# A hybrid decoder step: three feed-forwards of seven products, each behind the next group's mixing

## The chip, the cores and the metric

The kernel runs on one core of a Trainium2 chip, as one launch. The metric is the device time of that launch in microseconds (us). A core has five engines that run side by side and wait for each other through semaphores: TensorE (PE) multiplies matrices into PSUM banks, VectorE (DVE) and ScalarE (ACT) do elementwise work and may read PSUM, GpSimd (POOL) does elementwise work in SBUF only, and SyncE (SP) issues the DMA transfers. Each engine takes its instructions in the order of its own queue.

## The reference

A prompt of 2048 tokens and a sample group of 8 sequences of 8 tokens go through one decoder layer with the same weights (width 1024, feed-forward width 4096):

```
h    = rmsnorm(x)
proj = h @ w_in                      # 1024 x 4096: q, k, v, gate of 4 retention heads and of 4 HGRN2 heads
o    = per-head gated recurrence, head rmsnorm, swish gate
x    = x + o @ w_out                 # 1024 x 1024
x    = x + square(relu(rmsnorm(x) @ w_up)) @ w_down     # 1024 x 4096 and back
y    = rmsnorm(x)
```

The recurrence is computed in chunks; the prompt's state goes from one token group to the next, so the groups are mixed in order. The outputs are `y`, and the states of both kinds of heads after the prompt and after each sample sequence.

All of it is float32. The large products are made with operands split in two parts, `hi` (rounded to the matrix engine's input format) and `lo` (the rest): hi·hi + hi·lo + lo·hi, three matmuls in place of one.

## The kernel before, in words

Tokens lie on the free axis, channels on the 128 partitions. The 2112 tokens are worked on in three groups (`GROUPS`): 512 prompt tokens, then the 64 sample tokens with 768 prompt tokens (832), then 768 prompt tokens. For each group come, in this order, the mixing (`mix`: input projection, recurrence, gates), the output projection, and the feed-forward. The whole is one long emission in program order; PE works through it without a gap where the other engines keep up.

**The order of the work** is written by hand. Every matmul of a projection, or every second one of a feed-forward, calls `tick()`. `later(n, fn)` and `at(t, fn)` put other work (splits, sums, evacuations, loads) into an agenda that is carried out n ticks on, between the matmuls. `flush()` empties the agenda. `plan_sums` fills a second list, `side`, whose times are ticks too.

**Weights** come as tiles of 128 x 1024 from one array. `weight()` loads a tile (L241) into a buffer `raw`, ACT makes its `hi` part (L277), DVE or POOL its `lo` part (L292). In the first group the parts of all mixing and output weights but four are stored to DRAM (L325, `kept`), and the later groups load them back ready-made (L261).

**Two ways to do the feed-forward.** Group 0 (512 tokens, one piece of 512 columns) multiplies every weight block by its tokens: 64 weight tiles of 24 matmuls (`ffn_first`, `up_first`, `down_first`; the matmul is L352). Groups 1 and 2 cut the operands into 2 x 2 quarters and make seven products in place of eight (`ffn`, `up`, `down`; the matmul is the helper at L1146). A quarter is half of the group's tokens wide, so the matmuls have 416 and 384 columns. The seven products need sums of weight quarters S1 to S4: `plan_sums` loads quarters (L1286), adds them on DVE (L1289) and stores the sums to DRAM (L1294), for the up weights during group 0's feed-forward and for the down weights during group 1's mixing. They also need sums of token quarters T1 to T4 (`block_sum`, L1347), and each operand must be split (`halve`: L1336 on ACT, L1340 on DVE).

In `down` the result of a product goes from PSUM to SBUF by `put` (L1550 on DVE). Of the seven products of an octet some continue in the PSUM banks of the one before (`first` is false in `OCTET`), so that PE may go on in a bank only after DVE has read it:

```
OCTET = (("A11", "B11", True, ("U",)), ("A12", "B21", False, ((0, 0),)), ("S1", "T1", True, ((1, 1),)),
         ("S4", "B22", False, ((0, 1),)), ("S3", "T3", True, ((1, 1),)), ("A22", "T4", False, ((1, 0),)),
         ("S2", "T2", True, ("U",)))
```

Each product of `down` takes two weight tiles (v = 0 and 1) with a PSUM tile of two banks each, 24 matmuls a tile. The hidden activations go to DRAM after `up` and come back in `down`.

**Memory.** Most temporaries are slabs of 832 columns, 42 of them. PSUM holds two two-bank tiles `pj` for the large products and four single banks `mm`.

**Samples.** The 64 sample tokens are the first columns of group 1. `sample_update` (L771, L774) multiplies the keys by the values masked by sequence, in plain float32, and adds the result to the eight states of a head.

Of the kernel before, what the change touches and what calls it, by code (L numbers as in the profile page):

```python
# [9 lines left out]
F32 = mybir.dt.float32  # L10
# [5 lines left out]
P = 128  # L16
D = 1024
# [11 lines left out]
SLAB = 832  # L29
NSLAB = 42  # L30
# [6 lines left out]
GROUPS = ((0, 0, 512), (NS, 512, 768), (0, 1280, 768))  # L37
# [4 lines left out]
W_UP0 = W_OUT0 + N_OUT  # L42
W_DN0 = W_UP0 + N_UP
NQ = FF // (4 * P)
NO = NQ // 2

W_UQ0 = W_DN0 + N_DN
W_DQ0 = W_UQ0 + N_UP
NW = W_DQ0 + N_DN

# [41 lines left out]
NCONST = C_SM + NSEQ  # L92
# [14 lines left out]
def constants():  # L107
# [6 lines left out]
    for h, g in enumerate(GAM):  # L114
        dec = np.where(s <= t, g ** np.maximum(t - s, 0), 0.0) * sc
        c[:, C_RM + h * P:C_RM + (h + 1) * P] = dec
        c[:, C_RS + h * P:C_RS + (h + 1) * P] = np.where(same, dec, 0.0)
        c[:, C_GQ + h * P:C_GQ + (h + 1) * P] = g ** (t + 1.0)
        c[:, C_GS + h * NS:C_GS + (h + 1) * NS] = g ** (np.arange(NS) % SLEN + 1.0)
        c[:, C_KS + h] = sc * g ** (P - 1.0 - s[:, 0])  # L120
        c[:, C_KSS + h] = np.where(s[:, 0] < NS, sc * g ** (SLEN - 1.0 - s[:, 0] % SLEN), 0.0)
    c[:, C_SM:C_SM + NSEQ] = (s // SLEN == np.arange(NSEQ)[None, :])
# [31 lines left out]
def lay_out_weights(w_in, w_out, w_up, w_down):  # L154
# [14 lines left out]
    for ps in (range(0, H - 1), range(H - 1, H)):  # L169
        bl = [wo[kind, p, :, n] for n in N_ORDER for p in ps for kind in (1, 0)]  # L170
        for j in range(0, len(bl), 8):
            w[i] = np.stack(bl[j:j + 8], 1).reshape(P, WT)
            i += 1
    wu = w_up.reshape(KB, P, FF // P, P)
    for f in range(FF // P):
        w[i] = wu[:, :, f].transpose(1, 0, 2).reshape(P, WT)
        i += 1
    wd = w_down.reshape(8, 4, P, 4, 256)
    for f in range(8):
        for n in range(4):  # L180
            w[i] = wd[f, :, :, n].transpose(1, 0, 2).reshape(P, WT)
            i += 1
# [25 lines left out]
class Kernel:  # L208
# [43 lines left out]
    def weight(self, i):  # L252
        n = len(self.stream)
        while self.w_next < min(i + 1 + self.ahead, n):
# [39 lines left out]
    def plan_stream(self):  # L294

        self.stream = [("w", j) for j in range(W_UP0)]
        up = [[("w", W_UP0 + 4 * t + i) for i in range(4)] for t in range(NQ)]
        dn = [[("w", W_DN0 + 4 * t + i) for i in range(4)] for t in range(NQ)]
        self.stream += up[0]
        for t in range(NQ):  # L300
            self.stream += (up[t + 1] if t < NQ - 1 else []) + dn[t]
        self.n_first = len(self.stream)
# [3 lines left out]

        for g in range(1, len(GROUPS)):
            self.stream += [("p" if j >= N_MADE else "w", j) for j in range(W_UP0)]
# [3 lines left out]
            for o in range(NO):  # L312
                for k, (name, *_) in enumerate(LAST_OCTET if o == NO - 1 else OCTET):
                    end = g == len(GROUPS) - 1 and o == NO - 1 and k > 4
                    self.stream += [entry(name, ("d", o, v), W_DQ0 + 4 * (2 * o + v), not end and (2 * k + v) % 5 in (1, 3))
                                    for v in range(2)]

    def next_weight(self):
# [3 lines left out]
        if N_MADE <= i < W_UP0:  # L322
# [16 lines left out]
    def proj(self, g, blocks, acts, pieces=None):  # L339
# [3 lines left out]
        self.n_proj += 1  # L343
        if self.spread and self.n_proj % 3:
            pj = self.mm().unsqueeze(1)
        else:
            pj = self.pj.tile([P, 2, 512], F32, tag="pj", name="pj")
# [31 lines left out]
    def build(self):  # L379
        nc, tc, I = self.nc, self.tc, self.I  # L380
        with ExitStack() as ctx:
# [11 lines left out]
            self.ordered, self.spread, self.n_proj = True, False, 0  # L393
# [49 lines left out]
            for i, g in enumerate(gs):  # L443
                nxt = gs[i + 1] if i + 1 < len(gs) else None
                if i == 0:
                    self.mix(g)
                    self.plan_sums(sums[:NQ - 1], [90 + 200 * j for j in range(NQ - 1)])

                    self.spread = True
                    self.out_proj_first(g)  # L450
                    self.ffn_first(g, nxt)
                    self.spread = False
                    continue
                if i == 1:
                    self.finish_first(gs[0])

                    self.plan_sums(sums[NQ - 1:], [141 + 200 * (j // 2) + 85 * (j % 2) for j in range(2 * NO)])
                else:
                    self.finish(gs[i - 1])
                self.mix(g)  # L460
                self.out_proj(g)
                while self.side:
                    self.side.popleft()[1]()
                self.ffn(g, nxt)
# [64 lines left out]
    def norm_in(self, g, start=False):  # L529
# [71 lines left out]
        else:  # L601
            for kb in range(KB):
                self.later(5 * kb, piece, kb)
        t0 = 60 if start else 5 * KB
# [103 lines left out]
    def values(self, g, p, b):  # L708
# [7 lines left out]
        while left:  # L716
# [5 lines left out]
            for i, s in enumerate(part):  # L722
# [9 lines left out]
                if g.ns and s == 0:  # L732
                    b["vs"] = pair
# [29 lines left out]
    def sample_update(self, v, kt, s0, which, h, decay):  # L763
# [3 lines left out]
        for i in range(2):  # L767
            vm = self.get()
            v3 = vm[:, :512].rearrange("p (s v) -> p s v", v=P)
            m = self.con[:, C_SM + 4 * i:C_SM + 4 * i + 4]  # L770
            nc.vector.tensor_tensor(out=v3, in0=v.unsqueeze(1).to_broadcast([P, 4, P]),  # L771
                                    in1=m.unsqueeze(2).to_broadcast([P, 4, P]), op=ALU.mult)
            ps = self.mm()
            nc.tensor.matmul(ps, kt, vm[:, :512], start=True, stop=True)  # L774
# [24 lines left out]
    def mixer(self, g, p, b, t0):  # L799
# [181 lines left out]
        def turn(key, src, sg, cscale):  # L981

            scale = None if cscale is None else con[:, cscale + p:cscale + p + 1]
            if sg == 2:
                x[key, 2] = self.get()[:, :P]
                self.transposes(src, [slice(0, P)], x[key, 2], None if cscale is None else con[:, C_KSS + p:C_KSS + p + 1])
# [42 lines left out]
        def sample_state(hd):  # L1029
            last = x["eb"][:, :NS].rearrange("p (s j) -> p s j", j=SLEN)[:, :, SLEN - 1]  # L1030
            self.sample_update(b["vs"][hd], x["kth" if hd else "ktr", 2], x["s0", hd], hd, p, last if hd else GAM[p] ** SLEN)
# [62 lines left out]
        if n0:  # L1094
            at(t - 14, sample_load, 0)
            at(t + 1, sample, 0)
# [54 lines left out]
    def residual(self, g):  # L1151
# [4 lines left out]
        for n in N_ORDER:  # L1156
# [4 lines left out]
        self.flush()  # L1161
        return part

    def out_proj_first(self, g):
        nc, T = self.nc, g.T
        part = self.residual(g)
        acts = g.oc[H - 1]
        g.acc, h2 = [part[n] for n in range(KB)], {}  # L1170
        for n in N_ORDER:
            pj = self.proj(g, self.take(2), acts)
            acc, hi, lo = g.acc[n], self.getr(), self.getr()
            nc.vector.tensor_tensor(out=self.v2(acc, g), in0=pj, in1=self.v2(acc, g), op=ALU.add)
            wf = self.vec[:, V_FFN + n:V_FFN + n + 1]
            nc.scalar.activation(hi[:, :T], acc[:, :T], AF.Copy, scale=wf)  # L1176
            self.later(7, lambda acc=acc, hi=hi, lo=lo, wf=wf: nc.vector.scalar_tensor_tensor(
                out=lo[:, :T], in0=acc[:, :T], scalar=wf, in1=hi.bitcast(F32)[:, :T], op0=ALU.mult, op1=ALU.subtract))
            h2[n] = (hi, lo)
        g.h2 = [h2[n] for n in range(KB)]  # L1180

    def scale_residual_first(self, g):


        nc, T = self.nc, g.T
        x = {"sum": None}

        def square(acc):
            x["sum"] = self.add_square(g, x["sum"], acc)

        def split():
            x["parts"] = self.halves(g, x["sum"])

        def mean():
            x["q"] = self.get()
            for (c0, c1), ps in zip(g.pieces, self.both_sums(g, x["parts"])):
                nc.vector.tensor_scalar(out=x["q"][:, c0:c1], in0=ps, scalar1=1.0 / D, scalar2=EPS,
                                        op0=ALU.mult, op1=ALU.add)

        def scale(acc):  # L1200
            nc.gpsimd.tensor_tensor(out=acc[:, :T], in0=acc[:, :T], in1=x["q"][:, :T], op=ALU.mult)

        def guard():
            self.last_guard(g, x["q"])

        for n, acc in enumerate(g.acc):
            self.later(7 * n, square, acc)
            self.later(120 + 7 * n, scale, acc)
        self.later(92, split)
        self.later(112, mean)  # L1210
        self.later(194, guard)

    def up_first(self, g):
        nc, T = self.nc, g.T
        u = []
        for _ in range(4):
            pj = self.proj(g, self.take(KB), g.h2)
            r, hi, lo = self.get(), self.getr(), self.getr()
            nc.scalar.activation(self.v2(r, g), pj, AF.Relu)
            nc.scalar.activation(hi[:, :T], r[:, :T], AF.Square)  # L1220
            nc.vector.tensor_tensor(out=r[:, :T], in0=r[:, :T], in1=r[:, :T], op=ALU.mult)
# [598 lines left out]
```

## Time and profile before

| what | value |
|---|---|
| median of 3 runs | 2559.0 us (2558.8 to 2559.46) |
| the profiled execution | 2557.37 us |
| its span, first to last instruction | 2555.3 us |
| PE busy | 2533.7 us, 99% |
| DVE busy | 1677.7 us, 66% |
| ACT busy | 1167.0 us, 46% |
| POOL busy | 694.3 us, 27% |
| DMA | 442.33 MB, mean 173 GB/s |
| granted TensorE clock | 0.999 |

The rows that the prediction shows come from these views. The groups of instructions give, for a line and a shape, the count, the busy time (time that two instructions share is not counted twice), the mean duration of one, and the idle time of the engine before them with what ended it. A matmul's own duration is longer than its distance to the next, because matmuls overlap; what one costs in a stream is read from the starts in the timeline, where a row is `start, duration, engine, line, operation, tile, shape, count`. The windows give busy time of PE, PE's weight load, DVE, ACT and POOL in a stretch with the number of instructions in brackets, then the granted clock, the mean busy share of the 16 DMA engines, and GB/s. The waits of PE give total, times and longest.

### The profile page before, as it was taken

The page shows a single profiled execution, that of the slowest core. Times are in us where ns is not written, and L with a number is a line of the kernel's source. Part 1 is how long each engine was busy: PE and PEld are TensorE (multiplying, and loading weights), DVE is VectorE, ACT ScalarE, POOL GpSimd, SP SyncE. Part 2 cuts the span into 40 slices and gives each one's busy share as a digit, 9 for nine tenths or more (in the row PEclk, how much of TensorE's full clock was granted, in tenths as well). Part 3 has the DMA queues.
Part 4 walks back from the last instruction along what each step waited for, and adds up shares of the span by engine and source line. Part 5 has one row for each costly group of instructions (what it writes and reads, how often), then busy time and mean ns, then how long its engine had stood idle before and what let it go on. Part 6 is the DMA issues. An engine that isn't in the chain of part 4 may idle for free. (4 is left out here: it accounts for less than half of the span.)

```text
span 2555.3 us, 37138 instructions
## 1 busy us (share of the span) xinstructions
PE 2533.7 (99%) x14691; PEld 2401.3 (94%) x14691; DVE 1677.7 (66%) x2135; ACT 1167.0 (46%) x1570; POOL 694.3 (27%) x443
## 2 busy tenths in 40 slices
PE   8999999999999999999999999999999999999998
PEld 7888888888999999999999999999999999999998
DVE  6777775556657666665646978875456465549787
ACT  6776532325334434344434444544444354345444
POOL 4333241111324243202222322243243012222220
PEclk9999999999999999999999999999999999999999
DMA  7666854564264545644557555442222325565452
GB/s 269 217 220 225 291 198 173 189 215 133 91 231 149 198 170 167 244 132 161 169 169 245 188 173 180 145 153 83 109 106 96 120 85 188 174 215 205 173 181 91
DMA packets 146173, 442.33 MB, mean 173 GB/s; under 512 B 14672, under 2 KB 36176, under 8 KB 146000
## 3 DMA queue, kind: packets, MB, share of 16 engines
q1 hardware_dynamic: 145856, 439.94, 49.8%
q8 instruction: 116, 1.90, 0.3%
q14 instruction: 57, 0.47, 0.1%
q10 hardware_dynamic: 144, 0.02, 0.0%
HBM read 331.11 MB, written 108.79 MB: 172 GB/s over the span
## 5 line engine op out<-in xcount | busy, mean ns | idle before, releaser
L352 PE MATMUL pj<-slab,hi 128*128 128x416 f32 (+2 forms) x2844 | 740.1, 363 | 6.4 <-ACT hi L277 6.0
L277 ACT CAST hi<-raw 128x1024 fp32r<-128x1024 f32 x330 | 347.7, 1054 | 666.6 <-PE pu L1146 185.4
L352 PEld LDWEIGHTS pj<-slab,hi 128*128 128x128 f32 x2844 | 512.8, 188 | 39.3 <-ACT hi L277 6.3
L292 POOL TENSOR_TENSOR lo<-raw,hi 128x1024 fp32r<-128x1024 f32 x92 | 247.6, 2691 | 852.5 <-ACT hi L277 791.7
L1146 PE MATMUL pd<-slab,hi 128*128 128x416 f32 (+1 forms) x1776 | 464.8, 342 | 2.0 <-DVE slab L1550 2.0
L352 PE MATMUL pj<-slab,lo 128*128 128x416 f32 (+2 forms) x1422 | 434.4, 364 | 0.6 <-DVE lo L292 0.5
L292 DVE TENSOR_TENSOR lo<-raw,hi 128x1024 fp32r<-128x1024 f32 x238 | 301.7, 1268 | 199.5 <-ACT hi L277 199.0
L1146 PE MATMUL pu<-slab,hi 128*128 128x416 f32 (+1 forms) x1600 | 408.4, 342 | 0.0
L1146 PEld LDWEIGHTS pd<-slab,hi 128*128 128x128 f32 x1776 | 326.8, 188 | 4.9 <-issue 1.8
L1146 PE MATMUL pd<-slab,lo 128*128 128x416 f32 (+1 forms) x888 | 305.2, 344 | 0.0
L1146 PEld LDWEIGHTS pu<-slab,hi 128*128 128x128 f32 x1600 | 294.1, 188 | 1.5
L352 PEld LDWEIGHTS pj<-slab,lo 128*128 128x128 f32 x1422 | 259.5, 188 | 17.7 <-issue 1.9
L1146 PE MATMUL pu<-slab,lo 128*128 128x416 f32 (+1 forms) x800 | 264.2, 343 | 0.0
L352 PE MATMUL mm<-slab,hi 128*128 128x512 f32 x740 | 229.5, 390 | 0.0
L728 PE MATMUL pjv<-hi,slab 128*128 128x256 f32 x1088 | 212.4, 287 | 1.4 <-ACT slab L738 1.4
L1340 DVE TENSOR_TENSOR slab<-slab 128x832 fp32r<-128x832 f32 (+1 forms) x144 | 162.9, 1149 | 36.8 <-ACT slab L1336 17.6
L728 PEld LDWEIGHTS pjv<-hi,slab 128*128 128x128 f32 x1088 | 174.3, 190 | 3.8 <-ACT slab L738 2.2
L1336 ACT CAST slab<-slab 128x832 fp32r<-128x832 f32 (+1 forms) x144 | 122.5, 862 | 115.0 <-DVE slab L1347 83.0
L1146 PEld LDWEIGHTS pd<-slab,lo 128*128 128x128 f32 x888 | 166.6, 188 | 0.5
L352 PEld LDWEIGHTS mm<-slab,hi 128*128 128x128 f32 x740 | 138.5, 188 | 29.2 <-ACT slab L1176 0.4
L728 PE MATMUL pjv<-lo,slab 128*128 128x256 f32 x544 | 153.8, 283 | 0.0
L1146 PEld LDWEIGHTS pu<-slab,lo 128*128 128x128 f32 x800 | 149.6, 188 | 0.5
(207 smaller groups left out, 3666.6 us busy)
## 6 DMA issues: line engine op xcount, KB each, us to landing
raw<-w SPq DMA_DIRECT2D x270, 512.0 KB, 4.2
u<-ld SPq DMA_DIRECT2D x32, 416.0 KB, 4.2
slab<-u SPq DMA_DIRECT2D x32, 416.0 KB, 5.5
u<-ld SPq DMA_DIRECT2D x32, 384.0 KB, 4.6
slab<-u SPq DMA_DIRECT2D x32, 384.0 KB, 5.7
ld<-x SPq DMA_DIRECT2D x16, 416.0 KB, 6.4
ld<-x SPq DMA_DIRECT2D x16, 384.0 KB, 4.3
raw<-su1S SPq DMA_DIRECT2D x8, 512.0 KB, 4.6
```

Of the source, the lines that this page charges most:

```text
L277: self.nc.scalar.copy(hi, raw)
L292: eng.tensor_tensor(out=lo, in0=self.second.pop(j), in1=hi.bitcast(F32), op=ALU.subtract)
L352: self.nc.tensor.matmul(pj[:, i, :T2], w, a[:, c0:c1], start=j == 0 and q == 0, stop=j == n - 1 and q == 2)
L728: nc.tensor.matmul(pj[:, i * 256:(i + 1) * 256], a[:, s:s + C], ww, start=kb == 0 and q == 0, stop=kb == KB - 1 and q == 2)
L1146: self.nc.tensor.matmul(*a, **k)
L1336: self.nc.scalar.copy(hi[:, :g.T], B[name][:, :g.T])
L1340: self.nc.vector.tensor_tensor(out=lo[:, :g.T], in0=B[name][:, :g.T], in1=hi.bitcast(F32)[:, :g.T], op=ALU.subtract)
```

## The change

- The groups become 640 prompt tokens, 64 sample tokens with 640 prompt tokens (704), and 768 prompt tokens. Every group is cut into two pieces, so that the matmuls have 320, 352 and 384 columns. Slabs are 768 columns wide, and there are 44.
- All three feed-forwards use the seven products; the functions of the first group's own feed-forward and its weight copies are gone.
- The order becomes: mixing 0, output projection 0, mixing 1, output projection 1, feed-forward 0, mixing 2, output projection 2, feed-forward 1, feed-forward 2. Since a feed-forward no longer follows its own group's output projection, the residual goes to DRAM (`g.res`, L1219 of the changed kernel) and is loaded back twice (`quarter`, L1227): once to make the operands (`prepare`), once for the running sum (`scale_residual`).
- The sums of weights are made in mixing 0 (4 sets), in mixing 1 (8 sets), and in feed-forward 0 (3 sets, at 150, 350 and 760 ticks of it).
- `raw` has three buffers; up to the end of feed-forward 0 weight tiles use these alone.
- The update of the sample states: the hi part, the lo part and the hi part of 32 tokens are stacked on 96 partitions, so that one matmul in the fast format takes the place of one in plain float32; the values are moved there by small DMAs, the keys by transposes (`sample_values`, `sample_keys`).

The work is the same otherwise. The core of the diff:

```diff
-SLAB = 832
-NSLAB = 42
+SLAB = 768
+NSLAB = 44
...
-GROUPS = ((0, 0, 512), (NS, 512, 768), (0, 1280, 768))
+GROUPS = ((0, 0, 640), (NS, 640, 640), (0, 1280, 768))
...
-            while self.w_load <= j or j >= self.n_first and self.w_load <= j + 2 and self.w_load < n:
+            while self.w_load <= j or j >= W_UQ0 and self.w_load <= j + 2 and self.w_load < n:
...
-                k, later = self.w_load, self.w_load >= self.n_first
-                raw = self.raws[k] = self.wp.tile([P, WT], F32, tag="sum" if later and k % 3 else "raw", name="raw",
-                                                  bufs=4 if later and k % 3 else 2)
+                k, later = self.w_load, self.w_load >= self.n_sums
+                other = later and k % 7 % 2
+                raw = self.raws[k] = self.wp.tile([P, WT], F32, tag="sum" if other else "raw", name="raw",
+                                                  bufs=4 if other else 3)
...
+        mixing()
+        feed_forward()
+
+        self.n_sums = len(self.stream)
+        mixing()
+        feed_forward()
+        feed_forward(True)
...
-            for i, g in enumerate(gs):
...
+            self.plan_sums(sums[:H], [96 + 110 + 184 * j for j in range(H)])
+            self.mix(gs[0])
+            self.out_proj(gs[0], 1, lambda: self.norm_in(gs[1], pace=12))
+
+            self.plan_sums(sums[H:], [141 + 192 * (j // 2) + 85 * (j % 2) for j in range(2 * H)]
+                           + [192 * (H + 1) + t for t in (150, 350, 760)])
+            self.mix(gs[1])
+            self.out_proj(gs[1], 3, lambda: self.prepare(gs[0], 12))
+            self.ffn(gs[0], lambda: self.norm_in(gs[2], pace=8))
+            self.finish(gs[0])
+            self.mix(gs[2])
+            self.out_proj(gs[2], 3, lambda: self.prepare(gs[1], 12))
+            self.ffn(gs[1], lambda: self.prepare(gs[2], 8))
+            self.finish(gs[1], pace=6, wait=110, each=8)
+            self.ffn(gs[2], None, 100)
...
+    def sample_values(self, g, v):
+
+        nc, out = self.nc, []
+        for i in range(2):
+            r, w = self.load(), self.getr()
+            for t in range(3):
+                nc.sync.dma_start(r[32 * t:32 * t + 32, :2 * P], v[32 * i:32 * i + 32])
+            nc.scalar.copy(w[:96, :2 * P], r[:96, :2 * P])
+            nc.vector.tensor_tensor(out=w[64:96, :2 * P], in0=r[64:96, :2 * P], in1=w.bitcast(F32)[64:96, :2 * P], op=ALU.subtract)
+            out.append(w)
+        return out
+
+    def sample_keys(self, src, scale):
+
+        nc, out = self.nc, []
+        ps = self.mm(2 * P)
+        r = self.get()
+        nc.scalar.copy(r[:, :192].rearrange("p (i n t) -> p i n t", i=2, n=3),
+                       src[:, :NS].rearrange("p (i t) -> p i t", i=2).unsqueeze(2).to_broadcast([P, 2, 3, 32]))
+        for i in range(2):
+            nc.tensor.transpose(ps[:96, i * P:(i + 1) * P], r[:, 96 * i:96 * i + 96], self.ident)
...
-            nc.tensor.matmul(ps, kt, vm[:, :512], start=True, stop=True)
+            nc.tensor.matmul(ps, kt[:, i * P:(i + 1) * P], vm[:96, :512], start=True, stop=True)
...
+    def out_proj(self, g, when, beside):
+
+        nc = self.nc
+        part = self.residual(g, when, beside)
+        g.res = self.dp.tile([P, KB, g.T], F32, name=f"res{g.i}")
+        for n in N_ORDER:
+            pj = self.proj(g, self.take(2), g.oc[H - 1])
+            acc = self.v2(part[n], g)
+            nc.vector.tensor_tensor(out=acc, in0=pj, in1=acc, op=ALU.add)
+            nc.sync.dma_start(g.res[:, n], part[n][:, :g.T])
+        self.flush()
+
+    def quarter(self, g, v, m, h, into):
+
+        n, w = 4 * m + 2 * v, g.T // 2
+        self.nc.sync.dma_start(self.pair(g, into), g.res[:, n:n + 2, h * w:(h + 1) * w])
+
+    def prepare(self, g, pace):
+
+        g.B, g.ops = [{}, {}], [{}, {}]
...
+        for j, (v, m, h) in enumerate((v, m, h) for v in range(2) for m in range(2) for h in range(2)):
+            x = {}
+            first, second = self.halve(g, g.B[v], QUARTER[m, h], g.ops[v])
+            self.later(pace * j, load, x, v, m, h)
+            self.later(pace * j + 14, weigh, x, v, m, h)
+            self.later(pace * j + 16, first)
+            self.later(pace * j + 20, second)
...
         for k, (h, v, m) in enumerate((h, v, m) for h in range(2) for v in range(2) for m in range(2)):
-            self.later(110 + 20 * k, square, v, m, h)
-            self.later(350 + 20 * k, scale, v, m, h)
+            self.later(wait + 90 + 20 * k, load, v, m, h)
+            self.later(wait + 110 + 20 * k, square, v, m, h)
+            self.later(wait + 350 + 20 * k, scale, v, m, h)
...
-                if last and k % 7 == 3 and nxt is not None:
-                    self.norm_in(nxt)
+                if last and k % 7 == 2 and nxt is not None:
+                    nxt()
```

More of the change, by code (lines that the diff above doesn't have):

```diff
@@ L342, in proj @@
         T2 = pieces[0][1] - pieces[0][0]
[L343 to L347, printed above, removed]
+        pj = self.pj.tile([P, 2, 512], F32, tag="pj", name="pj")
         n = len(blocks)
@@ L1149, in matmul, with residual @@
             self.tick()
-    def residual(self, g):
+    def residual(self, g, when, beside):
         self.cut_heads(g, H - 2)
@@ L1155, in residual @@
         part = {}
-        for n in N_ORDER:
+        for j, n in enumerate(N_ORDER):
+            if j == when:
+                beside()
             x = self.x_block(g, n)
@@ L1182, in scale_residual_first @@
[L1182 to L1211, printed above, removed]
@@ L1624, in ffn, with finish @@
         self.flush()
-    def finish(self, g, hs=(0, 1), last=False):
+    def finish(self, g, hs=(0, 1), last=False, pace=4, wait=51, each=5):
         nc, T, T2 = self.nc, g.T, g.T // 2
```

221 lines of the change are left out of this document (59 added, 162 removed).

## The prediction

> **What bounds the kernel now.** I read the page's busy line first, then the waits of PE, then the windows, and last the starts of PE's matmuls.
>
> ```profile
> PE 2533.7 (99%) x14691; PEld 2401.3 (94%) x14691; DVE 1677.7 (66%) x2135; ACT 1167.0 (46%) x1570; POOL 694.3 (27%) x443
> ...
> PE pj L352 <- ACT hi L277: 6.0, 1, 6.0
> PE pd L1146 <- DVE slab L1550: 2.0, 3, 1.3
> PE pjv L728 <- ACT slab L738: 1.4, 4, 0.4
> ```
>
> PE is busy 99% of the span. Its one long wait is the start, 6.0 us until the first operands are there; the next are 2.0 us in three pieces, all in the last feed-forward, and 1.4 us in the mixing. So the time is the sum of PE's matmuls, and the change is worth what it takes from that sum, less what it brings in waits.
>
> What a matmul costs in a stream is read from starts in the timeline (512, 416, 384 and 256 columns):
>
> ```profile
> 10.35 0.61 PE L352 MATMUL pj<-slab,hi 128*128 128x512 f32 x2
> 13.07 0.61 PE L352 MATMUL pj<-slab,hi 128*128 128x512 f32 x2
> ...
> 1400.30 0.53 PE L1146 MATMUL pd<-slab,hi 128*128 128x416 f32 x2
> 1409.37 0.53 PE L1146 MATMUL pd<-slab,hi 128*128 128x416 f32 x2
> ...
> 2299.95 0.51 PE L1146 MATMUL pu<-slab,hi 128*128 128x384 f32 x2
> 2307.23 0.51 PE L1146 MATMUL pd<-slab,hi 128*128 128x384 f32 x2
> ...
> 999.87 0.41 PE L728 MATMUL pjv<-hi,slab 128*128 128x256 f32 x2
> 1002.03 0.40 PE L728 MATMUL pjv<-hi,slab 128*128 128x256 f32 x2
> ```
>
> Between the first two lie 4 threes of matmuls, so one takes 2.72/12 = 0.2267 us. For 416 it is 9.07/48 = 0.1890, for 384 7.28/42 = 0.1733, for 256 2.16/18 = 0.1200. Three of the four lie on one line, 0.1200 + 0.000417 per column above 256; 416 should have 0.1867 by it and has 0.0023 more. No matmul here has 320 or 352 columns. 320 is a multiple of 64 like the three, so 0.1467; 352 is an odd multiple of 32 like 416, so 0.1600 + 0.0023 = 0.1623, with 0.1600 as the other end.
>
> **The change part by part.**
>
> *The large products.* The counts:
>
> ```profile
> L352 PE MATMUL pj<-slab,hi 128*128 128x512 f32 x796 | 258.6, 399 | 6.4 <-ACT hi L277 6.0 <-ACT slab L738 0.4
> L352 PE MATMUL mm<-slab,hi 128*128 128x512 f32 x740 | 229.5, 390 | 0.0
> L352 PE MATMUL pj<-slab,hi 128*128 128x416 f32 x1024 | 248.2, 357 | 0.0
> L1146 PE MATMUL pd<-slab,hi 128*128 128x416 f32 x896 | 241.2, 350 | 0.0
> L1146 PE MATMUL pu<-slab,hi 128*128 128x416 f32 x800 | 210.2, 350 | 0.0
> L1146 PE MATMUL mm<-slab,hi 128*128 128x416 f32 x112 | 30.1, 350 | 0.0
> ```
>
> With half as many `lo` matmuls beside them, group 0 has 1.5 x 1536 = 2304 of 512 columns, and a group on seven products 1.5 x 2832 = 4248, of 416 and, by the same code, of 384. Before: 2304 x 0.2267 + 4248 x 0.1890 + 4248 x 0.1733 = 522.3 + 802.9 + 736.2 = 2061.4 us. After: 4248 x (0.1467 + 0.1623 + 0.1733) = 2048.8. The change is worth 12.6 us; 22.4 if 352 lies on the line. The eighth product saved in group 0 goes for the most part into the fixed share of a matmul, which three narrow groups pay more often.
>
> [...]
>
> *The sample states.*
>
> ```profile
> 843.17 1.88 PE L774 MATMUL mm<-slab 128*128 128x512 f32 x4
> 844.48 1.12 PE L352 MATMUL pj<-slab,hi 128*128 128x416 f32 x3
> ```
>
> Each plain float32 matmul has two records, so two take 1.31 us, one 0.655. In the fast format one takes 0.2267: 16 x 0.428 = 6.9 us less. Eight more transposes cost at most the 0.12 of a 256-column matmul each, 1.0. Gain 5.9. The values come by DMAs issued 18 ticks before the matmul; a late one would hold PE, at most 4 heads x 1.3 (the longest wait above) = 5 us. I take 0, since those ticks are 36 matmuls or more, some 6 us.
>
> *DVE behind PE in `down`.* Here lies the loss. The rows: one wait in the timeline; two windows as long as a product; the sums over such windows of `down` at 384 and at 416 columns; two groups of DVE.
>
> ```profile
> 2371.85 0.59 PE L1146 MATMUL pd<-slab,hi 128*128 128x384 f32 x2 [1.26 <-DVE slab L1550]
> ...
> 2364.88:2373.20 8.32, 6.69 (x38) 6.11 (x37) 8.32 (x8) 2.07 (x3) 3.08 (x1) 1.00 0.19 69
> 2373.20:2381.52 8.32, 7.96 (x46) 7.67 (x45) 8.23 (x9) 5.65 (x7) 3.15 (x1) 1.00 0.41 140
> ...
> sum 249.60, PE 247.59 PEld 246.18 DVE 212.87 ACT 116.45 POOL 63.36; mean PE 8.25 PEld 8.21 DVE 7.10 ACT 3.88 POOL 2.11
> ...
> sum 272.10, PE 272.10 PEld 269.59 DVE 223.12 ACT 129.67 POOL 70.71; mean PE 9.07 PEld 8.99 DVE 7.44 ACT 4.32 POOL 2.36
> ...
> L292 DVE TENSOR_TENSOR lo<-raw,hi 128x1024 fp32r<-128x1024 f32 x238 | 301.7, 1268 | 199.5 <-ACT hi L277 199.0 <-PE pu L1146 0.3
> L1289 DVE TENSOR_TENSOR raw<-raw 128x1024 f32<-128x1024 f32 x60 | 87.8, 1464 | 0.4
> ```
>
> A window of 8.32 us shows 48 matmuls and two at its edges; these two show 38 and 46 of 50, so 16 x 0.1733 = 2.8 us are lost, with DVE full. `put` is late there, and the next product, which continues in the same bank, stands behind it. DVE is 85.3% busy over `down` at 384 columns, with that loss, and 82.0% at 416, with none. Of 28 products of 48 matmuls (233 and 254 us) that is 199 and 208 us of DVE work. It falls by 9 us for 32 columns while PE's time falls by 19 to 21, since the 34 weight splits that DVE has in a `down` (43 us) don't shrink. So at 352 columns 190 us stand against 218 (87%), at 320 181 against 197 (92%). Drawn on from 0 at 82.0% and 2.8 at 85.3%, the losses are some 4.3 and 8.5; with the 2.8 of the last group 15.6, 12.8 more than before. Moreover the third set of sums in feed-forward 0 (760 ticks in; `down` starts at 684) falls into the full first octet: 4 x 1.464 = 5.9. The bounds are -2.8 (another order on DVE loses nothing) and +18.7. I take 2.8 in every group, since 87% lies next to the row that has it, and half of the set: 5.6 + 2.9 = +8.5.
>
> *The mixing.* In mixing 0 DVE's elementwise work and PE's columns both grow by a quarter. The sums of weights add 16 x 1.464 = 23 us of DVE there; mixing 1 keeps its 32 sums on a shorter stretch. PE's longest wait in the mixing is the 1.4 us of the first fence; I take 0, with 5 as the upper end.
>
> *Transfers.* The residual (24 stores, 48 loads), group 0's activations and the extra weight tiles bring some 67 MB to the 442. Most densely they lie in output projection 0:
>
> ```profile
> 250.00:300.00 50.00, 50.00 (x248) 41.78 (x248) 38.57 (x68) 23.29 (x41) 3.31 (x2) 1.00 0.92 329
> raw<-w SPq DMA_DIRECT2D x270, 512.0 KB, 4.2
> ```
>
> The first row is the same place before: 329 GB/s at a share of 0.92, so 358 when full, and PE without a gap. After, there are 9 weight tiles, each loaded (0.52 MB) and stored as two parts (1.05; 14.2 MB in all), this group's x (2.6), the next group's x and tables (3.6), the residual (2.6) and a set of sums (4.2): 27 MB, 76 us at 358 GB/s. PE has 384 x 0.1467 = 56 us there and the last head's recurrence beside it. Between 0 and 20 us could show; I take +1, near the row, since weights come two tiles (14 us) early. On SP the residual's stores wait for DVE's additions, and feed-forward 0's loads are queued behind them; five of its tiles are asked for before, some 30 us of PE work. Those tiles have three buffers where the seven-product groups had six: one is needed again after 3 x 3.52 = 10.6 us; 4.2 to land (the second row) and 1.3 for the `lo` part leave 5.1 for ACT's half and the waits between. I take 0, with 5 as the upper end. Elsewhere the activations' transfers hide beside PE as in the two groups that have them. The start waits for tiles a quarter wider: between 0 and 1.5 (a quarter of 6.0); I take 0.6.
>
> *ACT and POOL.* 45 more `hi` parts and 47 more `lo` parts on POOL lie beside PE; ACT was at 46%, POOL at 27%.
>
> *The sum.* -12.6 - 5.9 + 8.5 + 1 + 0.6 = -8.4 us. The profiled execution took 2557.4 (its span 2555.3 and 2.1 around it), so 2549.0; the median of the runs lies 1.6 above it, so 2551 us, 0.3% less.
>
> **The rivals.**
>
> *A: 352 columns cost what the line says* (0.1600), and the set of sums finds room: -9.8 - 2.9, so 2538. For it speaks the line, on which three of the four widths lie; against it the row of 416.
>
> *B: slower, by `put`.* A group's `down` has 22 weight tiles that continue in a bank which DVE must have read, and the time for that is one tile: 4.16 us at 384 columns, 4.54 at 416, 3.52 at 320 and 3.90 at 352. Before, three of 44 waited, 2.0 us in all, 0.67 each. If each of the 44 of groups 0 and 1 waited so, it would be 29.5 us in place of my 5.6: 2575. It decides (slower by over 0.2%) from 28 of the 44 on. Beside it stands a cost that doesn't shrink with the columns, seen on one line and shape:
>
> ```profile
> 2305.23 2.34 DVE L1347 TENSOR_TENSOR slab<-slab 128x768 f32<-128x768 f32 x1
> ...
> 2319.88 0.95 DVE L1347 TENSOR_TENSOR slab<-slab 128x768 f32<-128x768 f32 x1
> ```
>
> The same sum takes 0.95 us or 2.34, and POOL has 22 weight splits in every `down`. [...]
>
> *C: the transfers of output projection 0 show.* 10 us more: 2561, no change that counts. For it the 27 MB; against it the 0.92 above without a gap.
>
> That the seven products aren't made in all groups is excluded by the program: its product matmuls are 4248 of each width.
>
> **How the numbers follow.** Forecast 0.40, with 2543 to 2557 as its own range; A 0.23, C 0.12, B 0.20, late weight tiles in feed-forward 0 or something else that makes it slower 0.05. What differs by under 0.2% (5 us) can't be told from no change here. Faster: A and most of the forecast, 0.23 + 0.36 = 0.59. Same: the rest of the forecast and most of C, 0.14. Slower: B, the other, a little of C, 0.27. The low end has both good bounds, 2551 - 9.8 - 8.5 - 2.8 = 2530; the high end is B's 2575.
>
> **What would show it.** Right: starts of 0.1467 and 0.162 us at 320 and 352; L1478 as the main wait of PE, under 12 us; PE busy 99%; no wait on L230 or L250 work around output projection 0; the sample matmul at 0.23. Wrong: waits of PE on L1478 over 20 us, or windows of output projection 0 near 370 GB/s with PE below full.

## The result, and the profile after

The changed kernel takes 2571.5 us (median of 6 runs, 2568.1 to 2572.3) against 2559.1 for the kernel before on the same chip: 1.0044 times as long, 95% interval 1.0034 to 1.0055. The forecast was 2551 us; the change makes the kernel 0.4% slower. The profiled execution took 2570.45 us with a span of 2568.7, 13.4 more than before.

From the page of the changed kernel:

```profile
span 2568.7 us, 41708 instructions
...
PE 2515.8 (98%) x16641; PEld 2487.5 (97%) x16641; DVE 1811.5 (71%) x2283; ACT 1249.6 (49%) x1702; POOL 742.5 (29%) x443
```

PE works 17.9 us less than before (2533.7), about what was forecast, but it is idle for 52.9 us of the span where it was idle for 21.6. The time went into waits, 31.3 us more of them. The waits of PE tell which (total, times, longest):

```profile
PE pd L1159 <- DVE slab L1478: 17.5, 16, 2.2
...
PE pd L1159 <- ACT slab L1256: 5.4, 3, 2.5
PE mm L787 <- DVE slab L784: 2.1, 4, 0.6
PE mm L489 <- DVE slab L483: 2.0, 1, 2.0
PE pj L341 <- DVE slab L1218: 1.6, 2, 0.9
...
PE pj L341 <- DVE slab L1175: 1.5, 1, 1.5
PE mm L549 <- DVE slab L579: 1.5, 1, 1.5
...
PE pd L1159 <- ACT hi L267: 1.1, 1, 1.1
```

L1478 is `put`. L267 and L282 make the hi and the lo part of a weight tile, L1256 and L1260 those of an operand, and L1267 a sum of token quarters. With the ACT waits on L1256 and L267, which are operands of the same products, and the 2.0 us of the column sums on L489 that are issued in the last octet of feed-forward 0, 26.0 us are waited in the three `down`s, where it was 2.0 before. By shape of the product, in the groups of instructions:

```profile
L1159 PE MATMUL pd<-slab,hi 128*128 128x384 f32 x880 | 223.3, 334 | 2.5 <-DVE slab L1478 2.5
L1159 PE MATMUL pd<-slab,hi 128*128 128x352 f32 x896 | 215.3, 322 | 6.7 <-DVE slab L1478 3.9 <-ACT slab L1256 1.7 <-ACT hi L267 1.1
...
L1159 PE MATMUL pd<-slab,hi 128*128 128x320 f32 x896 | 202.3, 314 | 14.8 <-DVE slab L1478 11.1 <-ACT slab L1256 3.7
```

The narrower the product, the longer PE waits. What DVE does meanwhile stands in the timeline of DVE, and beside it that of POOL (start, duration):

```profile
1034.13 3.04 DVE L1260 TENSOR_TENSOR slab<-slab 128x640 fp32r<-128x640 f32 x1
1037.09 0.81 DVE L1478 TENSOR_TENSOR slab<-pd,slab 128x640 f32<-128x640 f32 x1
...
1038.95 3.42 DVE L282 TENSOR_TENSOR lo<-raw,hi 128x1024 fp32r<-128x1024 f32 x1
1042.30 0.81 DVE L1260 TENSOR_TENSOR slab<-slab 128x640 fp32r<-128x640 f32 x1
1043.03 0.81 DVE L1478 TENSOR_TENSOR slab<-pd,slab 128x640 f32<-128x640 f32 x1
```

```profile
1033.46 3.02 POOL L282 TENSOR_TENSOR lo<-raw,hi 128x1024 fp32r<-128x1024 f32 x1 [4.91 <-ACT hi L267]
1038.66 2.64 POOL L282 TENSOR_TENSOR lo<-raw,hi 128x1024 fp32r<-128x1024 f32 x1 [2.17 <-ACT hi L267]
```

The same split on L1260 takes 0.81 us at 1042.30 and 3.04 at 1034.13, and the long one lies beside a lo part on POOL. The `put` queued behind the long one starts at 1037.09, when that is done, so it is late by the 2.2 us (3.04 - 0.81). At the other end stands PE; below are its rows, and then windows with the clock that it was granted just after a wait:

```profile
1043.99 0.53 PE L1159 MATMUL pd<-slab,hi 128*128 128x320 f32 x2 [2.19 <-DVE slab L1478]
...
1050.65 0.46 PE L1159 MATMUL pd<-slab,hi 128*128 128x320 f32 x2
...
1059.45 0.46 PE L1159 MATMUL pd<-slab,hi 128*128 128x320 f32 x2
...
1072.09 0.53 PE L1159 MATMUL pd<-slab,hi 128*128 128x320 f32 x2 [2.53 <-ACT slab L1256]
...
1074.29 0.73 PE L1159 MATMUL pd<-slab,hi 128*128 128x320 f32 x2
1074.83 0.47 PE L1159 MATMUL pd<-slab,lo 128*128 128x320 f32 x1
1075.09 0.73 PE L1159 MATMUL pd<-slab,hi 128*128 128x320 f32 x2
...
1884.80 0.49 PE L1159 MATMUL pd<-slab,hi 128*128 128x352 f32 x2
...
1891.57 0.49 PE L1159 MATMUL pd<-slab,hi 128*128 128x352 f32 x2
```

```profile
300.00:350.00 50.00, 48.83 (x347) 48.10 (x346) 44.64 (x72) 34.22 (x51) 1.83 (x1) 1.00 0.76 265
...
1072.00:1074.00 2.00, 1.91 (x11) 1.94 (x12) 2.00 (x3) 2.00 (x3) 0.00 (x0) 0.86 1.01 406
1074.00:1076.00 2.00, 2.00 (x9) 2.00 (x9) 2.00 (x4) 0.17 (x1) 0.00 (x0) 0.50 0.30 117
...
991.29:1214.90 223.61, 206.86 (x1356) 203.06 (x1355) 204.86 (x205) 108.82 (x133) 67.52 (x26) 0.98 0.66 226
1857.26:2080.56 223.30, 216.57 (x1345) 215.24 (x1345) 196.40 (x188) 111.19 (x134) 64.18 (x24) 1.00 0.56 190
2320.44:2560.00 239.56, 236.82 (x1357) 234.78 (x1356) 205.21 (x200) 111.24 (x129) 58.61 (x21) 1.00 0.46 155
```

Between 1050.65 and 1059.45 lie 20 threes of matmuls of 320 columns, so one takes 8.80/60 = 0.1467 us. After the wait of 2.53 us a three takes 0.80 us (1074.29 to 1075.09) instead of 3 x 0.1467 = 0.44, at a granted clock of 0.50. There are three such stretches of some 3.4 us in feed-forward 0's `down`, none in the body of the kernel before. The first window, with output projection 0 in it, is for later; the last three are the `down`s of 320, 352 and 384 columns (PE, PE's weight load, DVE, ACT, POOL, clock, DMA share, GB/s).

### The profile page after: what moved, and what is told of

Read it like the earlier page. It is cut to its first block, busy times and chain, and to the rows that moved or that the text cites. A ratio compares the mean times of both kernels' runs of the same rounds, so it can differ in the third digit from the quotient of the medians.

```text
span 2568.7 us, 41708 instructions
## 1 busy us (share of the span) xinstructions
PE 2515.8 (98%) x16641; PEld 2487.5 (97%) x16641; DVE 1811.5 (71%) x2283; ACT 1249.6 (49%) x1702; POOL 742.5 (29%) x443
## 4 chain that ended last, share of the span: by engine, by line
PE 82%; DVE 9%; issue 3%; ACT 2%; DMA 2%; POOL 0%; SPq 0%; DVEq 0%; ACTq 0%; POOLq 0%
PE pj L341 24%; PE pu L1159 22%; PE pd L1159 18%; PE pjv L711 6%; PE mm L1159 3%; PE mm L870 1%; DVE slab L1260 1%; DVE slab L1267 1%; DVE lo L282 1%; PE mm L1058 1%; PE po L1050 1%; DVE slab L1478 1%; PE po L1052 1%; PE mm L489 1%; DVE raw L1191 1%
## 5 line engine op out<-in xcount | busy, mean ns | idle before, releaser
L282 POOL TENSOR_TENSOR lo<-raw,hi 128x1024 fp32r<-128x1024 f32 x139 | 370.8, 2668 | 1071.6 <-ACT hi L267 989.4
L267 ACT CAST hi<-raw 128x1024 fp32r<-128x1024 f32 x375 | 393.9, 1050 | 574.0 <-PE pu L1159 197.2
L341 PE MATMUL pj<-slab,hi 128*128 128x320 f32 (+2 forms) x3072 | 661.8, 329 | 11.2 <-ACT hi L267 6.2
L1159 PE MATMUL pd<-slab,hi 128*128 128x320 f32 (+2 forms) x2672 | 640.9, 324 | 24.0 <-DVE slab L1478 17.5
L1159 PE MATMUL pu<-slab,hi 128*128 128x320 f32 (+2 forms) x2400 | 557.3, 322 | 0.2 <-DVE ld L1405 0.2
L1159 PEld LDWEIGHTS pd<-slab,hi 128*128 128x128 f32 x2672 | 466.9, 189 | 29.0 <-issue 13.1
L1159 PE MATMUL pd<-slab,lo 128*128 128x320 f32 (+2 forms) x1336 | 431.6, 323 | 0.0
L282 DVE TENSOR_TENSOR lo<-raw,hi 128x1024 fp32r<-128x1024 f32 x236 | 304.2, 1289 | 165.2 <-ACT hi L267 159.9
L341 PE MATMUL pj<-slab,lo 128*128 128x320 f32 (+2 forms) x1536 | 380.2, 328 | 0.0
L1159 PE MATMUL pu<-slab,lo 128*128 128x320 f32 (+2 forms) x1200 | 370.6, 322 | 0.0
L1260 DVE TENSOR_TENSOR slab<-slab 128x640 fp32r<-128x640 f32 (+2 forms) x216 | 249.7, 1174 | 34.8 <-PE pd L1159 18.2
L1256 ACT CAST slab<-slab 128x704 fp32r<-128x704 f32 (+2 forms) x216 | 164.4, 780 | 163.7 <-DVE slab L1267 136.2
L1478 DVE TENSOR_TENSOR slab<-pd,slab 128x640 f32<-128x640 f32 (+2 forms) x166 | 145.7, 880 | 39.0 <-PE pd L1159 38.7
L1267 DVE TENSOR_TENSOR slab<-slab 128x640 f32<-128x640 f32 (+2 forms) x120 | 122.7, 1040 | 3.3 <-PE pd L1159 3.1
```

The lines of the kernel that those rows point to most:

```text
L267: self.nc.scalar.copy(hi, raw)
L282: eng.tensor_tensor(out=lo, in0=self.second.pop(j), in1=hi.bitcast(F32), op=ALU.subtract)
L341: self.nc.tensor.matmul(pj[:, i, :T2], w, a[:, c0:c1], start=j == 0 and q == 0, stop=j == n - 1 and q == 2)
L1159: self.nc.tensor.matmul(*a, **k)
L1256: self.nc.scalar.copy(hi[:, :g.T], B[name][:, :g.T])
L1260: self.nc.vector.tensor_tensor(out=lo[:, :g.T], in0=B[name][:, :g.T], in1=hi.bitcast(F32)[:, :g.T], op=ALU.subtract)
```

## The experiments

Two theories. Theory 1: POOL's lo parts of weight tiles block DVE's instructions, and so `put`. Theory 2: at 320 and 352 columns DVE simply has too much work of its own, as the prediction's sum had it. The runs were taken on several chips, so what counts of a time is its ratio to the kernel before on the same chip.

**No lo part on POOL in `down`.**

```diff
-                                          not (end and o == NO - 1 and k > 4) and (2 * k + v) % 5 in (1, 3)) for v in range(2)]
+                                          False) for v in range(2)]
```

> The changed kernel, with every lo part of a weight tile in the three `down`s made by DVE instead of 65 of them by POOL. Theory 1 (POOL's split blocks DVE): over `down` of feed-forward 0 DVE is busy 204.9 of 223.6 us, and some 43 us of that are instructions that last 1.5 to 3.8 us instead of 0.8 to 1.2, each beside one of POOL's 22 splits. DVE takes over 22 x 1.14 = 25 us and loses the 43, so it falls to about 187 us; the waits of PE in the three `down`s fall from 26.0 to under 8 us and the half-clock stretches go: 2543 to 2553 us. Theory 2 (DVE simply has too much of its own work at 320 and 352 columns): 25 us more of it in each `down`, PE waits grow by 15 to 30 us in feed-forward 0 and by 5 to 20 in the other two: 2595 to 2640 us.

Measured: 2547.0 us, 0.9956 (0.9943 to 0.9968) of the kernel before. By the ratios that is some 22 us less than the changed kernel, for one line, and now faster than before. By the counts of POOL's instructions the edit moves 70 lo parts to DVE (24, 24 and 22 in the three `down`s), not 65. The waits in the three `down`s fall from 26.0 to 8.3 us (these two and 1.4 on column sums):

```profile
PE pd L1159 <- DVE slab L1478: 3.9, 3, 1.9
PE pd L1159 <- ACT slab L1256: 3.0, 1, 3.0
```

One of the three stretches at half clock is left. DVE's groups in `down` of feed-forward 0, first of the changed kernel, then of this one:

```profile
L1260 DVE TENSOR_TENSOR slab<-slab 128x640 fp32r<-128x640 f32 x52 | 59.0, 1158 | 3.9 <-ACT slab L1256 1.9 <-PE pd L1159 1.8
L282 DVE TENSOR_TENSOR lo<-raw,hi 128x1024 fp32r<-128x1024 f32 x33 | 45.3, 1372 | 2.5 <-ACT hi L267 2.3
L1478 DVE TENSOR_TENSOR slab<-pd,slab 128x640 f32<-128x640 f32 x55 | 44.5, 812 | 9.1 <-PE pd L1159 9.1
```

```profile
L282 DVE TENSOR_TENSOR lo<-raw,hi 128x1024 fp32r<-128x1024 f32 x57 | 71.9, 1261 | 3.0 <-ACT hi L267 2.2
L1478 DVE TENSOR_TENSOR slab<-pd,slab 128x640 f32<-128x640 f32 x55 | 44.9, 820 | 6.7 <-PE pd L1159 6.2
L1260 DVE TENSOR_TENSOR slab<-slab 128x640 fp32r<-128x640 f32 x52 | 41.8, 818 | 0.0
```

Without POOL beside it a split on L1260 takes 818 ns instead of 1158. `put`, which has one input in PSUM, takes the same, 812 and 820: it is late not because it is blocked but because it stands behind what is.

One number of theory 1 was wrong: DVE was to fall to 187 us and is at 197. The 43 us of the expectation were whole durations; the blocking in them was 34.2, since DVE took over 26.6 us of lo parts (71.9 - 45.3) and was busy 7.6 us less. That makes the run tell more. The windows of `down` in feed-forwards 0 and 1, and of two stretches of the first:

```profile
990.64:1200.29 209.65, 201.39 (x1357) 199.94 (x1356) 197.26 (x228) 108.68 (x133) 4.64 (x2) 0.99 0.71 241
1843.14:2059.68 216.54, 216.54 (x1347) 216.54 (x1345) 194.68 (x211) 111.24 (x134) 2.40 (x1) 1.00 0.60 195
...
990.64:1160.00 169.36, 169.36 (x1157) 169.36 (x1156) 159.76 (x186) 86.25 (x104) 0.00 (x0) 1.00 0.76 260
...
1160.00:1190.00 30.00, 21.74 (x131) 20.54 (x130) 28.54 (x35) 18.51 (x25) 0.00 (x0) 0.94 0.54 167
```

DVE is busy 94% and 90% of the two `down`s, where it was 92% and 88%; and PE waits 8.3 and 0.0 us, where it waited 16.8 and 6.7. A higher share, fewer waits: the share of DVE over a `down` isn't what decides. Up to 1160 us DVE is 94% busy and PE doesn't wait at all. The 8.3 us all lie between 1160 and 1190, beside the normalization of group 2, where POOL does nothing and DVE is 95% busy. So theory 1 accounts for 17.7 of the 26.0 us. The other 8.3 can't be POOL's; they fit theory 2 in that one octet, which isn't shown further.

**POOL's lo parts made twice.**

```diff
+            if eng is self.nc.gpsimd and (e[1][0] == "d" if e[0] == "s" else e[1] >= W_DQ0):
+                eng.tensor_tensor(out=raw, in0=raw, in1=hi.bitcast(F32), op=ALU.subtract)
```

> The changed kernel, with each of POOL's 65 splits in the three `down`s followed by a second one of the same size, whose result nothing uses. DVE has no more work of its own. Theory 1 (POOL's split blocks DVE): each costs DVE about 43/22 = 1.95 us again, 43 us in each `down`, where 15 to 35 us of DVE are idle: 40 to 100 us slower, 2610 to 2670 us, with more and longer waits on the line of `put`. Theory 2 (DVE's own work): POOL is busy 29%, nothing waits for it: within 4 us of the changed kernel, 2567 to 2575 us.

Measured: 2688.7 us, 1.0507 (1.0488 to 1.0527), above what theory 1 expected and far from theory 2. Window, DVE's groups and the first wait of PE (lines have moved by four: L1264 is L1260, L1482 is `put`):

```profile
992.72:1267.36 274.64, 222.19 (x1356) 215.62 (x1355) 257.23 (x205) 109.35 (x133) 135.73 (x50) 0.92 0.55 184
```

```profile
L1264 DVE TENSOR_TENSOR slab<-slab 128x640 fp32r<-128x640 f32 x52 | 79.0, 1542 | 2.8 <-ACT slab L1260 1.5 <-PE pd L1163 1.4
...
L1482 DVE TENSOR_TENSOR slab<-pd,slab 128x640 f32<-128x640 f32 x55 | 44.5, 812 | 9.5 <-PE pd L1163 9.5
```

```profile
PE pd L1163 <- DVE slab L1482: 86.9, 45, 4.7
```

DVE has the same 205 instructions and is busy 257.2 us instead of 204.9: 24 more instructions of POOL (50 for 26) cost DVE 52.4 us, 2.2 us each, of the 2.9 us that each lasts. The expectation took each as dear as 1.95, and left out what PE pays besides: its granted clock over this `down` is 0.92, and the same matmuls keep it busy for 222.2 us instead of 206.9.

**The third set of weight sums out of `down`.**

```diff
-                           + [192 * (H + 1) + t for t in (150, 350, 760)])
+                           + [192 * (H + 1) + t for t in (150, 350, 550)])
```

> The changed kernel, with the third set of weight sums of feed-forward 0 at 550 ticks instead of 760, that is in `up`, where DVE is busy 62%, instead of the first octet of `down`. If the set is what tips `down` over (the prediction gave it half of 5.9 us), the time falls by 3 to 6 us, to 2565 to 2568. If POOL's splits alone make the waits, the four sums only use idle time of DVE elsewhere: 0 to 2 us less, 2569 to 2571.

Measured: 2568.0 us, 1.0036 (1.0023 to 1.0050). The median is 3.5 us below the changed kernel's, but by the ratios it is 2 us, at the border of the second reading, and the intervals overlap, so the times settle neither. In the trace the waits on `put` do fall, from 17.5 us in 16 pieces, while a new one of 2.3 us comes up on the copy of the first product (L1475) and one of 1.5 us at the end of `up`; in all, the waits in `down` of feed-forward 0 go from 16.8 to 13.0 us:

```profile
PE pd L1159 <- DVE slab L1478: 10.9, 11, 1.9
...
PE pd L1159 <- ACT slab L1475: 2.3, 1, 2.3
```

**The stacked sample states alone**, in the kernel before.

```diff
-            nc.tensor.matmul(ps, kt, vm[:, :512], start=True, stop=True)
+            nc.tensor.matmul(ps, kt[:, i * P:(i + 1) * P], vm[:96, :512], start=True, stop=True)
```

with `sample_values`, `sample_keys` and the constants that belong to it.

> The kernel before, with the stacked update of the sample states alone. The prediction's step says 5.9 us less with no wait on the values (2553.2); with the waits of 2.1 us that the changed kernel has on the masked values, 3.8 us less (2555.3). If the small DMAs or the extra work of ACT and DVE cost as much as the matmuls save, no difference (2559).

Measured: 2554.1 us, 0.9984 (0.9975 to 0.9993), 4.0 us less by the medians. PE is busy for 6.3 us less than before (2533.7):

```profile
PE 2527.4 (99%) x14683; PEld 2399.6 (94%) x14683; DVE 1686.7 (66%) x2151; ACT 1169.0 (46%) x1586; POOL 689.2 (27%) x443
```

The saving is as forecast, and a part of it is given back in short waits: PE is idle for 25.2 us of the span where it was 21.6. In the changed kernel 2.1 us are on L784, DVE's product of values and mask, before which DVE is never idle. So the values' DMAs, which the prediction thought of, are not what is late.

**The sets of sums rearranged**, without POOL's lo parts in `down`: one set fewer in mixing 1, four in `up` of feed-forward 0.

```diff
-            self.plan_sums(sums[H:], [141 + 192 * (j // 2) + 85 * (j % 2) for j in range(2 * H)]
-                           + [192 * (H + 1) + t for t in (150, 350, 760)])
+            self.plan_sums(sums[H:], [141 + 192 * (j // 2) + 85 * (j % 2) for j in range(2 * H - 1)]
+                           + [192 * (H + 1) + t for t in (60, 220, 380, 540)])
```

> The run without POOL's splits in `down`, and besides the last set of weight sums of mixing 1 moved into feed-forward 0, whose four sets start at 60, 220, 380 and 540 ticks, all in `up`. Theory: in output projection 1 the last set's four stores stand on SP ahead of a load of x (issued at 764.5 us, landed at 772.7), and PE waits 1.2 to 1.5 us for the addition of that x; with the set gone PE doesn't wait there, and the transfers fit beside `up`, where the DMA engines are 70 to 80% busy: 1 to 4 us less than without POOL's splits alone, 2543 to 2546 us. Rival: `up` of feed-forward 0 gets too full of transfers, weight tiles come late and PE waits for hi parts: 2 to 10 us more, 2549 to 2557.

Measured: 2538.4 us, 0.9917 (0.9904 to 0.9931); some 10 us less than the first experiment by the ratios, more than expected. The wait on L1175 in output projection 1 (1.2 us there, 1.5 in the changed kernel) is gone, which was the point. Some 3 us of new waits come up in `up`, and in the last octet of feed-forward 0 the waits fall from 8.3 to 2.1 us, though nothing in that octet was edited; why is open.

**And the normalization of group 2 spread out, no lo part on POOL in the first four tiles of a feed-forward.**

```diff
-            self.stream += [("w", W_UQ0 + i, i % 2) for i in range(4)]
+            self.stream += [("w", W_UQ0 + i, False) for i in range(4)]
...
-            self.ffn(gs[0], lambda: self.norm_in(gs[2], pace=8))
+            self.ffn(gs[0], lambda: self.norm_in(gs[2], pace=10))
...
-                if last and k % 7 == 2 and nxt is not None:
+                if last and k % 7 == (1 if g.i == 0 else 2) and nxt is not None:
```

> As the run before it, and besides: the normalization of group 2 beside the last octet of feed-forward 0 starts one product earlier and takes 10 ticks a block instead of 8, and no split of the first four tiles of a feed-forward is POOL's. Theory: without POOL's splits the 8.3 us that PE still waits in `down` all lie between 1160 and 1190 us, where DVE has 16 instructions of that normalization within 40 us; spread over 50 us, half of it goes, and the 0.7 to 0.9 us waits on L1218 that stand beside a POOL split go: 3 to 7 us less, 2537 to 2543 us. Rival: it is the amount of DVE's work in that octet and not its spacing: within 2 us of the run before it, 2543 to 2548.

Measured: 2537.3 us, 0.9914 (0.9900 to 0.9927), the fastest of all. It can't be told from the run before it, so neither part is shown to gain. In its trace the two waits on L1218 (1.6 us in the changed kernel) are gone, as expected; in the last octet 3.1 us of waits stay, against 2.1 before the spreading, so nothing shows that the spacing of the normalization makes them.

**The kernel before with both**: stacked sample states, no lo part on POOL in `down`.

```diff
-                    self.stream += [entry(name, ("d", o, v), W_DQ0 + 4 * (2 * o + v), not end and (2 * k + v) % 5 in (1, 3))
+                    self.stream += [entry(name, ("d", o, v), W_DQ0 + 4 * (2 * o + v), False)
```

> The kernel before, with the stacked sample states and without POOL's splits in its two `down`s of seven products. At 416 and 384 columns DVE had time left beside PE: PE waited 0 and 2.0 us there. If the blocking matters only where DVE has no time left, only these 2.0 us can go: 2551 to 2554 us. If POOL's splits cost the kernel before as much as the changed one, 10 us or more would go: under 2545 us.

Measured: 2551.1 us, 0.9969 (0.9956 to 0.9981). The 2.0 us of waits on `put` are gone from its trace, and no more was there to gain. The same edit that takes some 22 us off the changed kernel takes 2.0 us of waits off the kernel before. By the ratios it is 4 us against the run with the samples alone, but those intervals overlap. The blocking itself was there before. In the kernel before, in `down` at 416 columns, a split on L1340 (the lo part of an operand) lasts up to 3.23 us where most take 1.02 (min/median/max in ns), and PE is busy throughout:

```profile
L1340 DVE TENSOR_TENSOR slab<-slab x52: 1011/1020/3227, 1397.0 to 1627.3; 128x832 fp32r<-128x832 f32 x52
...
1392.40:1647.90 255.50, 255.50 (x1356) 252.84 (x1355) 213.30 (x200) 119.09 (x133) 68.78 (x25) 1.00 0.54 184
```

With its 23 more lo parts in that `down`, 26.4 us, DVE is busy 5.9 us more, so the blocking was 20.5 us there against 34.2 at 320 columns, and the wider matmuls covered it.

## Why the prediction was wrong

*The large products: right, and better than forecast.* 320 columns take 0.1467 us. 352 take 6.77/42 = 0.1612 (1884.80 to 1891.57 above), between the two ends 0.1600 (rival A's) and 0.1623, so the products are worth 12.6 + 4248 x 0.0011 = 17 us less instead of 12.6. The busy time agrees: without POOL's lo parts PE is busy for 2509.5 us, 24.2 less than before, 6.3 of it from the samples, which leaves 18 for the columns, in spite of one stretch at half clock.

*The sample states: right in the mechanism.* 5.9 us were forecast. PE's busy time fell by 6.3 and the median by 4.0, since waits that the step put at nothing took the rest.

*DVE behind PE in `down`: this is the step that failed.* It said 8.5 us, bounded by 18.7, and it was 24.0 (26.0 - 2.0), with the half clock behind it that nothing in the step allowed for: three stretches of 3.4 us, of which half, 5.1 us, is lost. What failed in it is the measure. The loss was drawn as a line over DVE's busy share (82.0%, 85.3%, then 87% and 92%). The shares themselves came out close, 88% and 92%, but as shares of `down`s that the waits had made longer: at 320 columns DVE is busy 204.9 us, where 181 and 5.9 for the set were drawn on. And the first experiment has higher shares and fewer waits. What fits the traces is how long `put` can be held up, by one blocked instruction above all, against the time of one weight tile, which is the slack of the bank: 3.52 us at 320 columns, 3.87 at 352 (24 x 0.1612), 4.16 at 384, 4.54 at 416. A blocked instruction of 3.0 or 3.4 us and a `put` of 0.8 are past it at 320. At 384 the kernel before has 3.15 and 0.95, which just about reach it, and three short waits; at 416 the 3.23 and 1.02 stay below it, and PE never waits. The blocking grew besides: worked out as above, from the runs with and without POOL's lo parts, it is some 20 us at 416 and 384 columns, 29 at 352 and 34 at 320. That POOL's blocking makes most of the waits is shown by the first two experiments; that the slack is the limit is argued from these figures, and no run changes the slack alone. The row with 2.34 us beside 0.95 stood in the prediction, but the delay that such an instruction makes for the `put` behind it was counted in no step. Two readings in the step are off without changing it much: by its own figures PE's time falls by 15 us from 384 to 352 columns and by 21 to 320, not by 19 to 21 each time, and POOL has 24 weight splits in the `down`s of groups 0 and 1, 22 only in the last.

*Rival B* had the right line, and a chance of 0.20. The cost that it saw on one line and shape, 2.34 us for 0.95, doesn't shrink with the columns in the runs: over a `down` the blocking is some 20 us at 416 and 384 columns, 29 at 352 and 34.2 at 320. That it comes from POOL the two rows didn't show; the first two experiments do. It was wrong about the form. There are not 28 waits or more of 0.67 us each; there are 16 on `put` of 1.1 us on the mean, up to 2.2, and three on L1256, ACT's part of a sum that DVE makes (L1267). Its 2575 us is 3.5 above what came, in part by luck: its 29.5 us of waits stand for 24.0 of waits and 5.1 of half clock, which it didn't think of.

*The mixing, and the start.* The mixing's own waits are about the old ones. The start costs 0.2 us more and its first column sums 1.3 (L579: 1.5 where it was 0.2), against 0.6 allowed.

*Transfers: the right cost in the wrong place.* Output projection 0 runs at 265 GB/s and a share of 0.76 (300 to 350 us above), and no wait on a load stands there; rival C didn't come. In output projection 1 a load of x is issued late and lands late, 8.6 us after its issue, behind the stores of a set of sums on SP's queue:

```profile
764.46 0.92 SPq L230 DMA_DIRECT2D ld<-x  x1
```

```profile
773.12 0.89 DVE L1175 TENSOR_TENSOR slab<-pj,ld 128x704 f32<-128x704 f32 x1 [0.43 <-DMA ld<-x]
```

That is the 1.5 us on L1175. The raw buffers, 3 for 6, cost nothing that shows: in feed-forward 0, where they are three, PE waits for no hi part, and the 1.1 us on L267 are in feed-forward 1, where the sums' buffers are used besides.

*The sum.* Of the 21.4 us between 2549.0 and the 2570.45 of the profiled execution, 15.5 are waits in `down` beyond the forecast and 5 the half clock; the other waits (output projections, start, samples) are 7.3 us where 1.6 were allowed for. The columns and samples give about 5 back.

*The signs named.* Starts of 0.1467 and 0.162: seen. L1478 as the main wait, under 12 us: it is 17.5, between that and the 20 named as wrong. Busy 99%: 98. The sign was set on one line; the waits on ACT behind the same DVE should have been counted with it. The sample matmul at 0.23: in the trace of the changed kernel the next matmul starts after 0.23 us at seven of the 16 and after 0.26 to 0.34 at eight; the sixteenth is followed by a wait.

## What to carry to other kernels

A busy share is no measure of waits where one engine must answer within a fixed slack: compare the longest instruction that can stand ahead of the answer with that slack (here 3.04 us and a `put` of 0.81 against 3.52), and look at one instruction's spread in the timeline, not at its group's mean. Work that POOL takes off DVE can cost DVE more than doing it: in feed-forward 0's `down` DVE was given 24 more lo parts, 26.6 us (71.9 - 45.3), and was busy 7.6 us less than when POOL made them. A change that shortens the covering work has to be costed with the delays it used to cover. With that one line changed the changed kernel is at 0.9956 of the kernel before, but the kernel before with the stacked samples and the same line changed is at 0.9969, and the intervals overlap. The new order and widths are clearly ahead only with the sets of sums rearranged too, 0.9917.

## What the runs showed of the hardware that was not expected

In `down` of feed-forward 0, where DVE is nearly full, a lo part on POOL (2.7 us) costs DVE 1.4 us (34.2 us for 24 of them), and one made right after it 2.2 (52.4 us for 24 more). `put`, which reads PSUM, pays nothing (812, 820 and 812 ns in the three runs).

PE's granted clock falls to 0.50 for stretches of about 3.4 us, and in the kernel with POOL's work doubled also for twice and three times that (6.8 and 10.2 us). Not every long wait brings one: the wait of 2.19 us ahead of 1043.99 is followed by none, those of 1.80 and 1.98 us ahead of 1182.00 and 1201.95 are. The three stretches in the changed kernel's `down` start at 1073.44, 1182.67 and 1203.15 us, 32 and 6 times 3.413 us apart. If PE's idle time in that trace is summed in windows of 3.413 us in step with the stretches, the three windows right before them have 2.06, 1.80 and 1.98 us of it, and no other window in the body of the kernel has more than 1.70. The wait of 2.19 us lies across a border of these windows, at 1042.72, with 0.92 and 1.27 us on its two sides. That is one trace, and no limit is shown by it: in the last experiment a stretch follows a window with 1.29 us idle, and why is open. With POOL's work doubled the stretches within feed-forward 0's `down` add up to 44 us where they were 10, and the same matmuls keep PE busy 15 us longer (222.2 for 206.9).
